# Gates of a linear-attention head by Ln and Exp in place of a reciprocal, meta scores stacked in two standing tiles, and a head's output steps regrouped, in a two-layer encoder trunk

## The chip, the cores and the metric

The kernel runs on one core of a Trainium2 chip. The metric is the device time of one execution in microseconds (us), as the median of several runs; lower is better. The core has five engines that run side by side, each through its own instructions in the order in which they were laid down: TensorE (PE in the profile; its weight loads are shown as PEld), VectorE (DVE), ScalarE (ACT), GpSimd (POOL) and SyncE (SP), which here issues the DMAs. An instruction that waits for another engine's result holds up everything behind it on its own engine.

## The reference, cut to what matters

Two encoder layers work on a residual stream of 272 positions (256 tokens and 16 learned "meta" positions) by 2048 channels. In each layer one projection gives the inputs of two head groups: four heads of bidirectional gated linear attention (GLA) and sixteen heads of neighbourhood attention (NA) on a 4 x 64 grid. Their outputs are joined, projected, added to the stream and normalised; a squared-ReLU MLP with 8192 hidden channels and another normalisation follow. All is float32.

The change touches the end of a GLA head. With o the sum of the forward and backward scans of a head (256 channels) and r the gate's projection:

```python
o = o * lax.rsqrt(jnp.mean(jnp.square(o), axis=-1, keepdims=True) + LN_EPS) * norm_w.astype(f32)
o = o.reshape(B, L, GLA_HEADS * GLA_DV) * jax.nn.silu(r.astype(f32))
```

where silu(r) = r / (1 + exp(-r)).

## The kernel before, in words

**Layout.** Channels lie on the 128 partitions, positions along the free dimension. The stream is 16 tiles of 128 channels. Layer 1 needs all 272 positions; layer 2 drops the meta positions from most products and works on 256. A float32 product is made of a high and a low part of each operand, in the type float32r: `three` (L151) issues three matmuls for each block of 128 x 128 weights in layer 1 (L160 to L162), and two, the first 512 columns wide, in layer 2 (L156, L157).

**Weights.** Weights come from HBM in tiles of 128 x 1024 (512 KB). For each tile `made` (L137) issues a DMA on SP's queue, a cast to the high part on ScalarE (`wh`, L147) and a subtraction for the low part on VectorE (`wl`, L148). There are three buffers of each kind; a tile is prepared two tiles ahead of its use.

**What sets the order.** `by_m` (L190) computes four output blocks of 128 channels (index m), each of 16 weight blocks, that is two weight tiles. After the first tile of each block and after the block's eviction it calls `pump`. `pump` (L104) feeds two queues of Python generators, a foreground queue `fg` and a background queue `bg`: each call adds a credit to each, and for every whole credit it runs one generator to its next `yield`, which lays down that step's instructions behind the weight matmuls issued so far (the `issue_after` of L98). So a *step* is the code between two yields, a *rate* is the number of steps per call of `pump`, and the small matmuls of attention stand in groups between runs of 16 or 24 projection matmuls. A generator that ends costs no credit. Within what the steps allow, the recording layer still moves single instructions a few places on an engine.

**The stage around the change**, in `layer` from L262 on. The generator `gla()` (L479) is put in `bg`. Two groups of projections (8 blocks, 16 calls of `pump`) give r for the eight gates; here the background rate is `GLA_R` = 1.3. I call this the **gate stage**. Then come six groups for NA (24 blocks); for the first five (40 calls) the background rate is `GLA_NA` = 1.1; this is the **NA stage**. Before the sixth group whatever is left of `gla()` is issued at once (L271).

- `gla()` takes two steps to start, and then for each of four heads ten *levels* and an output part. A level is a distance class of position pairs: `gaps` (L438) lets GpSimd subtract cumulated decays (four operations, L447 to L450 or L457 to L464, recorded as L460), `operands` (L467) takes Exp on ScalarE (L471) and multiplies by q and k on VectorE (L476; L473 and L474 for the last level in layer 2), and TensorE makes the scores (L505, L498 for the last), which VectorE or ScalarE puts into the head's score tile `A` (L521, L519). `gaps` runs two levels ahead of the matmul and `operands` one, with three buffers. The scores of meta positions as keys go to a tile `Am` of 16 rows (L517).
- `gla_out` (L529) makes the head's output. Step 1: a tile `am` of 80 rows is cleared on GpSimd (L533) and `stack` (L211) puts the high part of `Am` in rows 0 to 15 and 64 to 79 on ScalarE (L214, two copies) and the low part in rows 32 to 47 on VectorE (L215). Steps 2 and 3: for each half e of the head three matmuls (L542, L543 with the values V, L544 with `am`) into a PSUM bank and a Square on ScalarE (L545). Step 4: the squares are added and split (L548, L208, L209). Step 5: their mean by two matmuls (L776) and the reciprocal square root `rs` by Ln, Exp and a Newton step (`newton`, L427). It then waits, step by step, until the head's two gates are there. Steps 6 and 7: for each half VectorE computes bank x weight x `rs` (L560), then x gate (L561), and the result is split (L208, L209).
- `ev_r` (L406) evicts a projection r: exp(-r) on ScalarE (L411), + 1 on GpSimd (L412), a copy of r on ScalarE (L414). `silu` (L417), in `fg`, takes the reciprocal on VectorE in two halves (L421), a step each, and then multiplies by r (L424). With its empty first step it costs three credits.
- `na_pair` (L590), in `fg` behind them, makes two NA heads in five steps: scores (L601, L605), softmax (L582 to L588), transposes of values (L622, L623) and of probabilities (L637, L638, L640, with the evictions L641 and L642), and output (L652, L657).

Of the kernel before, what the change touches and what calls it, by code (L numbers as in the profile page):

```python
# [2 lines left out]

# [15 lines left out]
NM = 16  # L19
L = T + NM  # L20
DEPTH = 2
ROWS, GW = 4, 64
GH, GDK, GDV = 4, 128, 256
# [8 lines left out]
EPS = 1e-5  # L32
TAU = 16.0
NEG = -1e30
GLA_R, GLA_NA, NORMS = 1.3, 1.1, (1.0, 0.6)
LEAD = 4


# [9 lines left out]
class Trunk:  # L48
# [18 lines left out]
    def consts(self):  # L67
        nc, c = self.nc, self.cp
        t = lambda n, s, d=F32: c.tile(s, d, name=n, tag=n)
# [19 lines left out]
            nc.scalar.copy(self.ones_r[n], self.ones[n])  # L89
        self.eps = t("eps", [P, 1])  # L90
        nc.gpsimd.memset(self.eps, EPS)
        self.one = t("one", [P, 1])
        nc.gpsimd.memset(self.one, 1.0)

# [311 lines left out]
    def ev_r(self, c, ps):  # L406

        nc, n = self.nc, self.n
        self.y[c] = self.pair(self.yp, "y", c)
        s = self.g2.tile([P, L], F32, name="rs", tag="rs")[:, :n]  # L410
        nc.scalar.activation(s, ps, AF.Exp, scale=-1.0)  # L411
        nc.gpsimd.tensor_scalar(s, s, 1.0, 1.0, ALU.mult, ALU.add)  # L412
        r = self.g2.tile([P, L], F32, name="rv", tag="rv")[:, :n]
        nc.scalar.copy(r, ps)  # L414
        self.fg.append(self.silu(c, s, r))

    def silu(self, c, s, r):  # L417
        yield
        half = self.n // 2
        for p in (slice(0, half), slice(half, self.n)):  # L420
            self.nc.vector.reciprocal(s[:, p], s[:, p])  # L421
# [57 lines left out]
    def gla(self):  # L479
# [4 lines left out]
        nc, n, full, g2 = self.nc, self.n, self.full, self.g2  # L484
        levels = (7, 0, 1, 2, 3, 4, 5, 6, 8, 9)
        todo = iter([(h, lv) for h in range(GH) for lv in levels])
        begun = [self.gaps(*next(todo)) for _ in range(2)]
        yield
        ahead = self.operands(*begun.pop(0))
        yield  # L490
        for h in range(GH):
            A = g2.tile([P, 6, P], F32, name="A", tag="A")
            Am = g2.tile([NM, L], F32, name="Am", tag="Am")
            for lv in levels:
                q, k = ahead
                ps = self.bank()
# [17 lines left out]
                if lv == 9:  # L514
                    if full:
                        nc.vector.tensor_copy(A[:, 2:6:3, :NM], ps[:, T:T + 2 * NM].rearrange("p (s c) -> p s c", s=2))
                    nc.scalar.copy(Am[:, :T], ps[:NM, :T])  # L517
                elif lv >= 7:
                    nc.scalar.copy(A[:, 0:5:4, :] if lv == 7 else A[:, 1:4:2, :], p2)  # L519
                else:  # L520
                    nc.vector.copy_predicated(A[:, 0:5:4, :], self.mask[:, lv:lv + 1, :].to_broadcast([P, 2, P]), p2)  # L521
# [5 lines left out]
            yield from self.gla_out(h, A, Am)  # L527

    def gla_out(self, h, A, Am):  # L529

        nc, n, g2 = self.nc, self.n, self.g2
        am = g2.tile([80, L], F32R, name="am", tag="am")[:, :n]
        nc.gpsimd.memset(am.bitcast(F32), 0.0)  # L533
        self.stack(Am[:, :n], am, NM, (0, 64), 32)
        yield
        af = A.rearrange("p s c -> p (s c)")
        os_ = []
        sq = g2.tile([P, 2, L], F32, name="sq", tag="sq", bufs=1)
        for e in range(2):
# [4 lines left out]
            nc.tensor.matmul(o, lhsT=self.VS[:, c], rhs=am, start=False, stop=True)  # L544
# [478 lines left out]
```

## Time and profile before

| what | value |
|---|---|
| median of 3 runs | 2427.86 us (2427.23 to 2428.85) |
| the profiled execution's own time | 2427.82 us |
| its span, first to last instruction | 2425.8 us |
| granted TensorE clock over the span | 0.997 |
| TensorE busy | 2394.4 us (99%) |
| VectorE busy | 1576.3 us (65%) |
| ScalarE busy | 1189.2 us (49%) |
| GpSimd busy | 285.7 us (12%) |
| all DMA | 417.46 MB, 172 GB/s |
| TensorE's share of the chain that ended last | 94% |

Layer 1 runs until about 1245 us, layer 2 from there. The gate stage of layer 1 lies at about 120 to 183 us and its NA stage behind it to about 340 us; in layer 2 the two lie at about 1357 to 1411 us and 1411 to 1570 us. How to read the views: the *waits* list sums, for an engine, the idle time ahead of its instructions by the instruction that ended it; the *chain* follows the work that ended last back from the end, at each place to what released it; the *windows* give the busy time of each engine in a stretch of the span; a *group* is all instructions of one line, engine and operation, with their number and mean time. A float32 matmul that is not of the type float32r is recorded as two, so the two score products of a level appear as four L505.

### The profile page before, as it was taken

To read this page: it belongs to the slowest core of one execution; us is meant where nothing else is said; L and a number is where in the kernel's file an instruction comes from. 1 tells how busy PE (TensorE), PEld (TensorE's weight loads), DVE (VectorE), ACT (ScalarE), POOL (GpSimd) and SP (SyncE) were. 2 spreads that over 40 slices of the span, in tenths; PEclk is the share of its full clock that TensorE was granted. 3 is DMA by queue.
4 is the path that set the end of the run, shared out by engine and by line. 5 is a ranking of instruction groups with operands and counts; after the bars stand their busy time and mean duration, and the time that the engine had idled before them with its cause. 6 is when DMAs were issued, how large, how long until landed. Compare 5 with 4: busy or idle time off the path is not lost.

```text
span 2425.8 us, 43082 instructions
## 1 busy us (share of the span) xinstructions
PE 2394.4 (99%) x17276; PEld 2270.6 (94%) x17276; DVE 1576.3 (65%) x2469; ACT 1189.2 (49%) x1962; POOL 285.7 (12%) x447
## 2 busy tenths in 40 slices
PE   9999999999999999999999999999999999999997
PEld 9999999999999999999999899999988888888886
DVE  6688777775544455546577787778866555666655
ACT  6555555564433344444456555555644333444443
POOL 1064420010000000000021444300200000000000
PEclk9999999999999999999999999999999999999998
DMA  7544444555555555555555444456566556556563
GB/s 243 165 133 155 145 133 158 172 179 175 174 175 174 175 177 174 177 175 173 176 168 186 144 156 150 136 156 191 184 190 184 190 189 187 189 185 189 186 189 129
DMA packets 118359, 417.46 MB, mean 172 GB/s; under 512 B 13388, under 2 KB 16332, under 8 KB 118160
## 3 DMA queue, kind: packets, MB, share of 16 engines
q1 hardware_dynamic: 118160, 414.72, 54.1%
q8 instruction: 135, 2.21, 0.4%
q14 instruction: 64, 0.52, 0.1%
HBM read 412.57 MB, written 2.10 MB: 171 GB/s over the span
## 4 chain that ended last, share of the span: by engine, by line
PE 94%; DVE 3%; issue 1%; ACT 1%; DMA 0%; POOL 0%; SPq 0%; ACTq 0%; DVEq 0%; POOLq 0%
PE mm L156 22%; PE mm L160 17%; PE mm L162 17%; PE mm L161 17%; PE mm L157 11%; PE mm L186 5%; PE bg L505 1%; DVE wl L148 1%; PE bg L652 1%; DVE acc L868 1%; PE bg L601 0%; POOL lev L460 0%; ACT wh L147 0%; PE bg L322 0%; PE bg L542 0%
## 5 line engine op out<-in xcount | busy, mean ns | idle before, releaser
L148 DVE TENSOR_TENSOR wl<-raw,wh 128x1024 fp32r<-128x1024 f32 (+1 forms) x772 | 946.0, 1226 | 654.6 <-ACT wh L147 646.2
L147 ACT CAST wh<-raw 128x1024 fp32r<-128x1024 f32 (+1 forms) x772 | 805.1, 1044 | 956.6 <-PE mm L161 405.6
L160 PE MATMUL mm<-x,wh 128*128 128x272 f32 (+2 forms) x2176 | 632.6, 291 | 0.0
L161 PE MATMUL mm<-x,wh 128*128 128x272 f32 (+2 forms) x2176 | 628.4, 289 | 0.0
L162 PE MATMUL mm<-x,wl 128*128 128x272 f32 (+2 forms) x2176 | 628.4, 289 | 0.0
L160 PEld LDWEIGHTS mm<-x,wh 128*128 128x128 f32 x2176 | 413.3, 190 | 1.4 <-issue 0.5
L162 PEld LDWEIGHTS mm<-x,wl 128*128 128x128 f32 x2176 | 410.6, 189 | 0.3
L161 PEld LDWEIGHTS mm<-x,wh 128*128 128x128 f32 x2176 | 410.0, 188 | 0.1
L156 PE MATMUL mm<-x,wh 128*128 128x512 f32 x1152 | 408.7, 397 | 0.0
L157 PE MATMUL mm<-x,wl 128*128 128x256 f32 x1152 | 324.5, 282 | 0.3 <-DVE wl L148 0.3
L156 PEld LDWEIGHTS mm<-x,wh 128*128 128x128 f32 x1152 | 217.7, 189 | 49.8 <-issue 0.6
L156 PE MATMUL mm<-y,wh 128*128 128x512 f32 x704 | 248.2, 393 | 0.1
L157 PEld LDWEIGHTS mm<-x,wl 128*128 128x128 f32 x1152 | 217.6, 189 | 0.8 <-DVE wl L148 0.8
L162 PE MATMUL mm<-y,wl 128*128 128x272 f32 x704 | 203.2, 289 | 0.0
L160 PE MATMUL mm<-y,wh 128*128 128x272 f32 x704 | 203.2, 289 | 0.0
L161 PE MATMUL mm<-y,wh 128*128 128x272 f32 x704 | 202.9, 288 | 0.0
L157 PE MATMUL mm<-y,wl 128*128 128x256 f32 x704 | 197.6, 281 | 0.5 <-DVE wl L148 0.5
L156 PE MATMUL mm<-u,wh 128*128 128x512 f32 x512 | 180.6, 393 | 0.0
L460 POOL TENSOR_TENSOR lev<-be 128x128 f32<-128x128 f32 (+1 forms) x256 | 151.9, 623 | 117.9 <-PE bg L505 49.8
L156 PEld LDWEIGHTS mm<-y,wh 128*128 128x128 f32 x704 | 131.8, 187 | 30.5 <-ACT wh L147 0.5
L162 PE MATMUL mm<-u,wl 128*128 128x272 f32 x512 | 147.8, 289 | 0.0
L160 PE MATMUL mm<-u,wh 128*128 128x272 f32 x512 | 147.8, 289 | 0.0
(234 smaller groups left out, 3327.9 us busy)
## 6 DMA issues: line engine op xcount, KB each, us to landing
raw<-in_wff SPq DMA_DIRECT2D x512, 512.0 KB, 3.6
raw<-in_win SPq DMA_DIRECT2D x190, 512.0 KB, 3.5
raw<-in_wout SPq DMA_DIRECT2D x64, 512.0 KB, 3.6
nb<-in_nab SPq DMA_DIRECT2D x16, 352.0 KB, 3.3
out<-acc SPq DMA_DIRECT2D x8, 256.0 KB, 2.2
xraw<-in_xT SPq DMA_DIRECT2D x7, 272.0 KB, 5.2
wraw<-in_wup SPq DMA_DIRECT2D x2, 392.0 KB
raw<-in_win SPq DMA_DIRECT2D x4, 128.0 KB, 2.8
```

Source lines behind the costliest of these rows:

```text
L147: nc.scalar.copy(wh[:, c], raw[:, c])
L148: self.wl = nc.vector.tensor_tensor(wl[:, c], raw[:, c], wh[:, c].bitcast(F32), ALU.subtract).ins
L156: mm(ps, lhsT=wh[:, c:c + P], rhs=x.both[:, :, :T], start=first, stop=False)
L157: mm(ps[:, T:], lhsT=wl[:, c:c + P], rhs=xh[:, :T], start=False, stop=last)
L160: mm(o, lhsT=wh[:, c:c + P], rhs=xh[:, :n], start=first, stop=False)
L161: mm(o, lhsT=wh[:, c:c + P], rhs=xl[:, :n], start=False, stop=False)
L162: mm(o, lhsT=wl[:, c:c + P], rhs=xh[:, :n], start=False, stop=last)
L186: self.nc.tensor.matmul(ps[m][:, :n], lhsT=parts[p][0][:, c:c + P], rhs=acts[j][parts[p][1]][:, :n], start=j + p == 0, stop=j == nk - 1 an ...
L460: tt = lambda o, x, y: nc.gpsimd.tensor_tensor(o, x, y, ALU.subtract)
L505: nc.tensor.matmul(ps[:, b], lhsT=k[:, b], rhs=q[:, r], start=True, stop=True)
L652: nc.tensor.matmul(r[hs], lhsT=(v2 if rest else v1)[:, t, hs], rhs=p2[:, t, :] if rest else p1[:, 2 * t + hh, :], start=rest, stop=not rest)
L868: return self.nc.vector.tensor_tensor(v, v, by[:, None, :].to_broadcast([P, m, n]), alu)
```

## The change

1. Gates. exp(-r) is capped at 1e38 as 1 is added (same GpSimd operation), and r is evicted negated. `silu` then takes 1/d as Exp(-Ln(d)) on ScalarE (scaled by 2^-64 inside the Ln, undone by the bias `down`), and refines it on VectorE by one Newton step that also multiplies by r: three operations. It takes two credits.
2. Two tiles `am0`, `am1` of the whole kernel part stand for all heads and are cleared once per layer; stacking moves into the step of the last level.
3. `gla_out` waits for its two gates first. One step then issues the six matmuls (both halves' V products, then both `am` products), the two Squares, and for each half bank x weight x gate on VectorE; the banks are read for the last time here. The last two steps multiply by `rs` from SBUF. An output part has five steps in place of seven.
4. Rates: `GLA_R` from 1.3 to 0.95, `GLA_NA` from 1.1 to 1.17.

```diff
-GLA_R, GLA_NA, NORMS = 1.3, 1.1, (1.0, 0.6)
+GLA_R, GLA_NA, NORMS = 0.95, 1.17, (1.0, 0.6)
+BIG = 1e38
...
+        self.down = t("down", [P, 1])
+        nc.gpsimd.memset(self.down, -64 * math.log(2))
...
-        s = self.g2.tile([P, L], F32, name="rs", tag="rs")[:, :n]
-        nc.scalar.activation(s, ps, AF.Exp, scale=-1.0)
-        nc.gpsimd.tensor_scalar(s, s, 1.0, 1.0, ALU.mult, ALU.add)
+        d = self.g2.tile([P, L], F32, name="rd", tag="rd")[:, :n]
+        nc.scalar.activation(d, ps, AF.Exp, scale=-1.0)
+        nc.gpsimd.tensor_scalar(d, d, BIG, 1.0, ALU.min, ALU.add)
         r = self.g2.tile([P, L], F32, name="rv", tag="rv")[:, :n]
-        nc.scalar.copy(r, ps)
-        self.fg.append(self.silu(c, s, r))
-
-    def silu(self, c, s, r):
-        yield
-        half = self.n // 2
-        for p in (slice(0, half), slice(half, self.n)):
-            self.nc.vector.reciprocal(s[:, p], s[:, p])
-            yield
-        gate = self.g2.tile([P, L], F32, name=f"gate{c}", tag=f"gate{c}", bufs=1)[:, :self.n]
-        self.nc.vector.tensor_tensor(gate, r, s, ALU.mult)
-        self.gate[c] = gate
+        nc.scalar.activation(r, ps, AF.Copy, scale=-1.0)
+        self.fg.append(self.silu(c, d, r))
+
+    def silu(self, c, d, r):
+
+        yield
+        nc = self.nc
+        y = self.g2.tile([P, L], F32, name=f"gate{c}", tag=f"gate{c}", bufs=1)[:, :self.n]
+        nc.scalar.activation(y, d, AF.Ln, scale=2.0 ** -64)
+        nc.scalar.activation(y, y, AF.Exp, scale=-1.0, bias=self.down)
+        yield
+        nc.vector.tensor_tensor(d, d, y, ALU.mult)
+        nc.vector.scalar_tensor_tensor(d, d, -2.0, y, ALU.add, ALU.mult)
+        nc.vector.tensor_tensor(y, d, r, ALU.mult)
+        self.gate[c] = y
...
+        ams = [g2.tile([80, L], F32R, name=f"am{i}", tag=f"am{i}", bufs=1) for i in range(2)]
+        for am in ams:
+            nc.gpsimd.memset(am.bitcast(F32), 0.0)
...
                     nc.scalar.copy(Am[:, :T], ps[:NM, :T])
+                    am = ams[h % 2][:, :n]
+                    self.stack(Am[:, :n], am, NM, (0, 64), 32)
...
-    def gla_out(self, h, A, Am):
+    def gla_out(self, h, A, am):
...
-        am = g2.tile([80, L], F32R, name="am", tag="am")[:, :n]
-        nc.gpsimd.memset(am.bitcast(F32), 0.0)
-        self.stack(Am[:, :n], am, NM, (0, 64), 32)
-        yield
+        while 2 * h + 1 not in self.gate:
+            yield
         af = A.rearrange("p s c -> p (s c)")
-        os_ = []
         sq = g2.tile([P, 2, L], F32, name="sq", tag="sq", bufs=1)
-        for e in range(2):
-            o = self.bank()[:, :n]
-            c = slice(h * GDV + e * P, h * GDV + e * P + P)
+        os_ = [(self.bank()[:, :n], slice(h * GDV + e * P, h * GDV + e * P + P)) for e in range(2)]
+        for o, c in os_:
             nc.tensor.matmul(o, lhsT=self.V[0][:, c], rhs=af[:, :n], start=True, stop=False)
             nc.tensor.matmul(o, lhsT=self.V[1][:, c], rhs=af[:, 384:384 + n], start=False, stop=False)
+        for o, c in os_:
             nc.tensor.matmul(o, lhsT=self.VS[:, c], rhs=am, start=False, stop=True)
+        on = []
+        for e, (o, c) in enumerate(os_):
             nc.scalar.activation(sq[:, e, :n], o, AF.Square)
-            os_.append(o)
-            yield
+            t = g2.tile([P, L], F32, name="on", tag="on")[:, :n]
+            nc.vector.scalar_tensor_tensor(t, o, self.vec[:, self.l, 64 + e:65 + e], self.gate[2 * h + e],
+                                           ALU.mult, ALU.mult)
+            on.append(t)
+        yield
...
-        while 2 * h + 1 not in self.gate:
-            yield
         for e in range(2):
             c = 2 * h + e
             hi, lo = (t[:, :n] for t in self.y[c])
-            o = g2.tile([P, L], F32, name="on", tag="on")[:, :n]
-            nc.vector.scalar_tensor_tensor(o, os_[e], self.vec[:, self.l, 64 + e:65 + e], rs, ALU.mult, ALU.mult)
-            nc.vector.tensor_tensor(o, o, self.gate[c], ALU.mult)
-            self.split(o, hi, lo)
+            nc.vector.tensor_tensor(on[e], on[e], rs, ALU.mult)
+            self.split(on[e], hi, lo)
```

More of the change, by code (lines that the diff above doesn't have):

```diff
@@ L1 @@
+import math
 from collections import deque
@@ L526, in gla @@
                 yield
[L527 to L529 removed]
+            yield from self.gla_out(h, A, am)
+    def gla_out(self, h, A, am):
         nc, n, g2 = self.nc, self.n, self.g2
[L532 to L535 removed]
+        while 2 * h + 1 not in self.gate:
+            yield
         af = A.rearrange("p s c -> p (s c)")
[L537 removed]
         sq = g2.tile([P, 2, L], F32, name="sq", tag="sq", bufs=1)
[L539 to L541 removed]
+        os_ = [(self.bank()[:, :n], slice(h * GDV + e * P, h * GDV + e * P + P)) for e in range(2)]
+        for o, c in os_:
             nc.tensor.matmul(o, lhsT=self.V[0][:, c], rhs=af[:, :n], start=True, stop=False)
             nc.tensor.matmul(o, lhsT=self.V[1][:, c], rhs=af[:, 384:384 + n], start=False, stop=False)
+        for o, c in os_:
             nc.tensor.matmul(o, lhsT=self.VS[:, c], rhs=am, start=False, stop=True)
+        on = []
+        for e, (o, c) in enumerate(os_):
             nc.scalar.activation(sq[:, e, :n], o, AF.Square)
[L546 to L547 removed]
+            t = g2.tile([P, L], F32, name="on", tag="on")[:, :n]
[3 more added lines that the diff above has]
+        yield
         nc.vector.tensor_tensor(sq[:, 0, :n], sq[:, 0, :n], sq[:, 1, :n], ALU.add)
```

## The prediction

> **What bounds the kernel now.** I read the page first, for the engines' shares:
>
> ```profile
> span 2425.8 us, 43082 instructions
> PE 2394.4 (99%) x17276; PEld 2270.6 (94%) x17276; DVE 1576.3 (65%) x2469; ACT 1189.2 (49%) x1962; POOL 285.7 (12%) x447
> ```
>
> TensorE is busy for all but 31.4 us, and the change takes no matmul from it. The time can fall only by idle time of TensorE, and only where the change reaches: gate and NA stage. So next came the windows of these stages: bounds, length, then busy time of TensorE, weight loads, VectorE, ScalarE and GpSimd. Layer 1 first (two lines), then layer 2:
>
> ```profile
> 120.00:183.00 63.00, 61.94 (x493) 61.25 (x493) 51.33 (x79) 31.95 (x55) 42.38 (x61) 1.00 0.43 137
> 183.00:340.00 157.00, 156.90 (x1316) 153.01 (x1316) 120.75 (x267) 90.62 (x214) 66.53 (x115) 1.00 0.45 146
> 1357.00:1411.00 54.00, 50.15 (x299) 43.56 (x298) 46.16 (x70) 31.22 (x57) 30.28 (x51) 1.00 0.46 143
> 1411.00:1570.00 159.00, 157.28 (x1201) 146.65 (x1199) 122.63 (x227) 90.92 (x199) 72.17 (x121) 1.00 0.47 147
> ```
>
> TensorE's idle time is 1.06 and 0.10 us in layer 1, 3.85 and 1.72 us in layer 2; the worst stage is the one where VectorE is busy for 46.16 of 54 us. The waits of TensorE in layer 2 (1344 to 1600 us) name the places:
>
> ```profile
> PE bg L544 <- ACT rs L411: 1.7, 1, 1.7
> PE bg L505 <- DVE lev L476: 1.2, 2, 1.0
> PE bg L652 <- DVE p L642: 0.8, 1, 0.8
> PE bg L776 <- ACT sp L208: 0.8, 1, 0.8
> PE bg L498 <- ACT rv L414: 0.6, 1, 0.6
> PE mm L157 <- DVE wl L148: 0.3, 1, 0.3
> ```
>
> Each is one event or two. Layer 1 has a single one, 1.06 us ahead of L544. An idle stretch costs more than itself, since the matmuls' overlap starts anew: from the matmul before to the one after, the V products that waited 1.06 us took 2.47 us and the same group without a wait 1.17, so 1.30 for 1.06. I add 0.2 us to each event (an estimate from this pair). Last, the chain at two of the places. Layer 2, the wait ahead of L505 at 1369.89 us:
>
> ```profile
> 1366.26 1.42 DVE wl L148
> 1367.68 0.86 DVE rs L421
> 1368.54 0.30 DVE A L521
> 1368.84 0.30 DVE jn L170
> 1369.14 0.61 DVE lev L476
> ```
>
> VectorE works without a pause, a reciprocal in the middle, and the level's operand L476 comes late. Layer 1, the wait ahead of L544, which starts at 153.77:
>
> ```profile
> 148.76 3.41 POOL lev L460 x4
> ...
> 152.75 0.41 ACT am L214
> ...
> 153.19 0.44 DVE am L215
> ```
>
> The stacking of `am` stands on ScalarE behind an Exp (L471, at 152.19) that waits for GpSimd.
>
> **The change part by part.**
>
> *Stacking.* Four of the eight clearings (L533, 0.32 us each on GpSimd) go, and stacking starts one step earlier. After the last level's matmul it needs ScalarE's Exp of the next level (L471, 0.63), `Am` (L517, 0.36), two copies (L214, 2 x 0.40) and the low part (L215, 0.42): 2.2 us, about 2.5 with the hand-overs. Where the V products come a whole call of `pump` later, TensorE covers this with 16 projection matmuls in layer 2 (eight pairs of 0.35 us by the starts of neighbours: 2.8 us) and four V products of 0.46 us each: 4.6 us. So the waits ahead of L544 go: 1.06 + 1.71 + 2 x 0.2 = **3.2 us**. The built order shows one head in each layer (the second) where the last level and the V products fall into one call; the cover there is 1.84 us and three or four projection matmuls, 2.2 to 2.5 us. Each can wait 0 to 1 us; I take 0.4 each, **+0.8**.
>
> *Gates and the gate stage's rate.* A gate now costs VectorE two reciprocals (L421, median 0.953) and a product (L424, 0.434): 2.34 us. New are three operations like L424, L432 and L561 (0.43): 1.29 us, so 16.8 us less over 16 gates. ScalarE gets Ln and Exp, priced by L429 and L430 at 0.42 to 0.48, so 0.9 us a gate and 14 us in all; it has 23 us free in layer 2's gate stage. The lower rate takes 16 x 0.35 = 5.6 steps out of that stage, each level 0.69 (L476) + 0.44 (L521) on VectorE: 6.3 us. VectorE then needs about 38 us there (46.2 - 6.3, less some 2 for seven or eight gates at 1.29 in place of five at 2.34), and TensorE 47.9 (50.15 less five levels of 0.45): 79% in place of 85%, with no level pair in one call, which was the case in the chain above. I let the waits on L476, L414 and L148 go (1.02 + 0.18 + 0.60 + 0.34, and 4 x 0.2: 2.9 us) but for 0.6 us: **-2.3**. If ScalarE's new pair holds up the weight casts instead, that is the slower rival. VectorE's relief is worth nothing by itself in layer 1, where TensorE hides it all.
>
> *A head's values in one step.* VectorE's count and kinds stay (L560, L561); ScalarE's Squares too. The banks come free some steps earlier; no wait of TensorE in the list is put down to L560, so that is worth 0. The six matmuls in a row cover the two PSUM reads (0.49 each). The mean's matmuls L776 waited 0.77 us and then 0.08 at 1447 us, where the split and the mean fell into one call of `pump`; in the new order no such pair is left. 0.85 and two restarts: **-1.2 us**. The wait for the gates ahead of the V products costs nothing: the second gate is there after about six calls, the first head ends after twelve.
>
> *More in the NA stage.* The foreground backlog of eight credits is gone (24 credits against 16 calls before, 16 now), so NA pairs start eight calls earlier, and their bias loads on SP's queue too; DMA engines are 0.47 busy, and no wait names them. Two starting steps, 40 levels and 20 output steps are 62, and the credits are 15.2 + 46.8 = 62, so the six steps that were issued at once ahead of the sixth group are spread; they had cost TensorE nothing. But calls with two level steps in the NA stage rise from two to five in layer 2. One such pair led to the wait of L652 (0.80): GpSimd's seven L460 in a row (4.13 us) held up an Exp, that the cast, that L148, that L642. In the new order these pairs stand where no transposes follow in the next call, so that event may go (-1.0 with its restart) or repeat (0.5 a pair by one event in two pairs, 3 more: +1.5). I take the middle, **+0.3**.
>
> *Fewer, longer groups.* A level standing alone adds 0.36 us to the projection's run (0.49 less the 0.126 of a projection matmul), behind another small group 0.45. Seven groups fewer: 7 x 0.09 = **+0.6**.
>
> Sum: -3.2 + 0.8 - 2.3 - 1.2 + 0.3 + 0.6 = **-5.0 us**. Against the profiled execution's 2427.82 that is 2422.8; its median differs by 0.04, so I leave it there.
>
> A rule that speaks against the change: the three new operations read two SBUF tensors each, the reciprocal one. In this trace L424, of that kind, goes from 0.415 to 0.675 us, and L412 on GpSimd from 0.404 to 1.397. The Trainium skill (GPSIMD Engine Reference, Specifications) says that GpSimd shares its SBUF interfaces with VectorE and contends with instructions that have two SBUF inputs; the spread of these rows agrees.
>
> **The rivals.**
>
> *Contention eats the relief (unchanged within 0.2%).* At 0.675 each, the new operations cost 2.0 us a gate and save 0.3. Then only the lower rate helps, and I keep half of the 2.3; GpSimd's levels get slower too, and the pair event repeats (+1.5 for +0.3): -5.0 + 1.15 + 1.2 = -2.65, **2425.2**. For it: 0.675 occurs. Against it: the median is 0.434, and GpSimd's share falls with the rate.
>
> *Waits return in the NA stage (also within 0.2%).* Stacking waits 1 us in both heads (+1.2 more) and the pair event repeats (+1.2 more): -5.0 + 2.4 gives **2425.2** as well. Against it: layer 1's pairs in the NA stage never idled TensorE.
>
> *All idle time goes.* The events are 6.56 us (1.06 + 1.71 + 1.20 + 0.80 + 0.85 + 0.60 + 0.34) and 9 restarts of 0.2: 8.4; less 0.6 for the groups, **2420.0**.
>
> *ScalarE becomes the bound: slower.* Ln waits for GpSimd's add, which stands behind a level's four L460 (2.58 us at 1523.95); behind Ln on ScalarE stands the next weight tile's cast. It decides from where the add ends more than about 2.8 us, half a projection block, after the eviction. At 1.5 us of starved TensorE for each of layer 2's eight gates, +12 - 5.0: **2435**. For it: ScalarE waits for L460 eight times in that stage, 11.0 us, up to 2.4. Against it: no wait of TensorE there went back to those, tiles are two ahead, and at 0.95 GpSimd has 2.0 to 2.9 us of level work for each 3.2 us call.
>
> That Ln and Exp would reload tables I leave out as a case: L429 and L430 alternate so already, and the trace has one ACT_TABLE_LOAD (1.28 us).
>
> **How the numbers follow.** About 0.2% (4.9 us) is what a measurement here can tell from no change. Forecast, -5 us and the neighbourhood down to all idle time gone: 0.50 for faster. The two rivals within 0.2%, and the forecast missed by a little: 0.43. ScalarE's bound: 0.07. The likeliest is 2422.8. The range takes in all idle time gone (2420.0) and, upward, the rivals at 2425.2 with the gate stage's 2.3 lost too: 2427.5.
>
> **What would show it.** In the new profile: no wait of TensorE ahead of L544 but in second heads; VectorE under 85% in layer 2's gate stage; TensorE's idle time there 1 us or less in place of 3.85; no L776 wait near 0.8. A wait of L156 or L157 on the cast or on L148 within the gate stage would show ScalarE's bound. New waits of L505 or L652 in calls with two levels would show the NA stage's. I am wrong if idle time in these stages stays at 6 us, or if TensorE's busy time moves by more than 1 us.

## The result and the profile after

The changed kernel takes **2439.18 us** (median of 4 runs, 2438.83 to 2439.64); the kernel before, beside it, 2427.55 (2427.09 to 2428.85). The ratio is 1.0047, 95% interval 1.003 to 1.0065: slower by 11.6 us. The forecast was 2422.8, so it is missed in sign and by 16 us.

The page of the profiled execution after: the span, the engines' busy times, and the shares of the chain that ended last.

```profile
span 2437.5 us, 43085 instructions
...
PE 2396.9 (98%) x17276; PEld 2273.1 (93%) x17276; DVE 1564.4 (64%) x2469; ACT 1199.8 (49%) x1994; POOL 302.6 (12%) x444
...
PE 89%; DVE 4%; POOL 3%; issue 2%; ACT 1%; DMA 0%; SPq 0%; ACTq 0%; POOLq 0%; DVEq 0%
```

The span is 11.7 us longer: TensorE's idle time rose from 31.4 to 40.6 us (+9.2) and its busy time by 2.5. VectorE lost 11.9 us of work, ScalarE gained 10.6, and GpSimd gained 16.9 although it has three instructions less (444 for 447). TensorE's share of the chain fell from 94 to 89%, and GpSimd, at 12% of the span, holds 3% of it. The windows of the same stretches as before show where:

```profile
120.00:183.00 63.00, 61.34 (x480) 60.13 (x479) 47.65 (x79) 39.04 (x73) 45.10 (x56) 1.00 0.42 138
183.00:340.00 157.00, 154.59 (x1286) 150.04 (x1285) 116.94 (x265) 88.33 (x212) 76.20 (x124) 1.00 0.43 139
1357.00:1411.00 54.00, 45.91 (x259) 39.27 (x257) 37.64 (x60) 31.51 (x63) 32.60 (x44) 0.97 0.43 141
1411.00:1570.00 159.00, 154.71 (x1164) 144.53 (x1162) 122.45 (x226) 93.28 (x203) 76.05 (x127) 1.00 0.46 145
```

TensorE's idle time in the four is 1.66, 2.41, 8.09 and 4.29 us, where it was 1.06, 0.10, 3.85 and 1.72: +9.7, where the whole span has +9.2. VectorE's share in layer 2's gate stage did fall, to 37.64 of 54 us, 70%. (The stretch is the same, but the projection matmuls that filled it before now run from 1360.95 to 1419.60 us; over these, VectorE is busy for 43.38 of 58.65 us, 74%.) So VectorE got its relief, and TensorE waited more.

Most of the rise in busy time goes with the waits too. The granted clock of the third line is 0.97 because of one stretch at half the clock, right behind TensorE's longest wait in the four (3.90 us), which ended at 1405.62 us. Here is that stretch, and then one of the same length behind it (the granted clock is the third number from the end):

```profile
1406.63:1410.04 3.41, 3.41 (x13) 2.93 (x12) 2.67 (x5) 2.26 (x6) 0.57 (x1) 0.50 0.23 71
1410.04:1413.45 3.41, 3.41 (x22) 3.01 (x21) 1.89 (x6) 2.44 (x5) 0.50 (x1) 1.00 0.35 144
```

In it TensorE runs 13 matmuls where it then runs 22; a pair of projection matmuls takes 0.64 us from start to start where it then takes 0.35. That is about 1.7 us lost (an estimate, half of 3.41), the greater part of the 2.5. The kernel before has no such stretch except over the last 16 us of the span, where all the kernels have one. In the traces of all 20 kernels here, each wait of TensorE of 2.0 us or more in these stages has a stretch at half the clock around or behind it, 3.41 or 6.83 us long; of the waits from 1.75 to 1.96 us some have one; shorter ones have none, the longest of before (1.71 us) among them.

The waits of TensorE in layer 2 (1344 to 1600 us):

```profile
PE bg L553 <- DVE am L219: 5.8, 2, 3.9
PE mm L161 <- DVE wl L152: 3.2, 3, 1.8
PE bg L662 <- DVE p L652: 2.4, 3, 1.1
PE bg L550 <- ACT A L531: 1.0, 1, 1.0
```

Lines have moved: the `am` product L544 is now L553, `wl` L152, the subtractions L460 are L467, GpSimd's step of a gate L412 is L416, Ln and Exp of a gate are L426 and L427, an output of NA L662. Projection matmuls in the gate stage now wait for the weights' low part, as the prediction's slower rival would have it, and the `am` products wait in layer 2's first two heads. Two chains explain the two kinds. First the wait of 1.84 us ahead of L161 at 1382 us:

```profile
1376.93 2.50 POOL lev L467 x4
...
1379.46 0.64 ACT lev L478
...
1380.12 0.94 DVE lev L483
1381.06 0.56 DVE rd L429
...
1382.73 0.33 DVE jn L174
1383.06 1.15 DVE wl L152
```

It starts with a level's subtractions on GpSimd; their Exp, the product, and then the gate's three operations and the weights' low part follow. Second, the wait of 1.86 us of layer 2's second head, from 1456.9 us on:

```profile
1454.77 2.46 POOL lev L467 x4
...
1457.26 0.63 ACT lev L478
1457.88 0.30 ACT am L218
...
1458.21 0.43 DVE am L219
```

Here the subtractions of a later level stand ahead of the stacking: ScalarE has that level's Exp ahead of the two `am` copies in its order, and waits for it. Both begin on GpSimd, so I looked at GpSimd's own order. Its timeline in layer 2's gate stage (in brackets the idle time before an instruction and what ended it):

```profile
1366.59 1.26 POOL L416 TENSOR_SCALAR rd<-rd 128x256 f32<-128x256 f32 x1 [1.06 <-ACT rd L415]
1367.93 4.44 POOL L467 TENSOR_TENSOR lev<-be 128x128 f32<-128x128 f32 x8
1375.78 1.07 POOL L416 TENSOR_SCALAR rd<-rd 128x256 f32<-128x256 f32 x1 [3.41 <-ACT rd L415]
1376.93 4.39 POOL L467 TENSOR_TENSOR lev<-be 128x128 f32<-128x128 f32 x8
1383.60 1.52 POOL L416 TENSOR_SCALAR rd<-rd 128x256 f32<-128x256 f32 x1 [2.27 <-ACT rd L415]
```

GpSimd idles 3.41 us with subtractions queued, since the gate's step stands ahead of them and waits for an eviction; and the step then takes 1.07 us or more. The subtractions at 1376.93 are those of the first chain. The matmul that freed the buffer of the first four of them had ended at 1372.39 us, 4.5 us earlier.

### The profile page after: what moved, and what is told of

Read it like the earlier page. It is cut to its first block, busy times and chain, and to the rows that moved or that the text cites. A ratio compares the mean times of both kernels' runs of the same rounds, so it can differ in the third digit from the quotient of the medians.

```text
span 2437.5 us, 43085 instructions
## 1 busy us (share of the span) xinstructions
PE 2396.9 (98%) x17276; PEld 2273.1 (93%) x17276; DVE 1564.4 (64%) x2469; ACT 1199.8 (49%) x1994; POOL 302.6 (12%) x444
## 4 chain that ended last, share of the span: by engine, by line
PE 89%; DVE 4%; POOL 3%; issue 2%; ACT 1%; DMA 0%; SPq 0%; ACTq 0%; POOLq 0%; DVEq 0%
PE mm L160 21%; PE mm L164 16%; PE mm L166 16%; PE mm L165 16%; PE mm L161 11%; PE mm L190 6%; POOL lev L467 2%; DVE wl L152 1%; PE bg L515 1%; DVE acc L878 1%; PE bg L662 1%; PE bg L611 0%; PE bg L326 0%; ACT ns L594 0%; ACT wh L151 0%
## 5 line engine op out<-in xcount | busy, mean ns | idle before, releaser
L152 DVE TENSOR_TENSOR wl<-raw,wh 128x1024 fp32r<-128x1024 f32 (+1 forms) x772 | 946.4, 1227 | 663.0 <-ACT wh L151 654.4
L161 PE MATMUL mm<-x,wl 128*128 128x256 f32 x1152 | 325.2, 282 | 3.2 <-DVE wl L152 3.2
L161 PEld LDWEIGHTS mm<-x,wl 128*128 128x128 f32 x1152 | 218.1, 189 | 4.2 <-DVE wl L152 4.2
L161 PE MATMUL mm<-y,wl 128*128 128x256 f32 x704 | 197.9, 282 | 0.5 <-DVE wl L152 0.5
L467 POOL TENSOR_TENSOR lev<-be 128x128 f32<-128x128 f32 (+1 forms) x256 | 157.3, 646 | 82.7 <-DVE be L351 45.5
```

The lines of the kernel that those rows point to most:

```text
L152: self.wl = nc.vector.tensor_tensor(wl[:, c], raw[:, c], wh[:, c].bitcast(F32), ALU.subtract).ins
L161: mm(ps[:, T:], lhsT=wl[:, c:c + P], rhs=xh[:, :T], start=False, stop=last)
L467: tt = lambda o, x, y: nc.gpsimd.tensor_tensor(o, x, y, ALU.subtract)
```

## The experiments

Each run was compared with the kernel before on the same chip (2427.4 to 2427.9 us there), so times of runs from different chips compare to within about 0.5 us. All of them:

| run | base | time, us | ratio, 95% interval |
|---|---|---|---|
| e1 old rates | after | 2445.76 | 1.0077 (1.0062 to 1.0092) |
| e2 old gates | after | 2431.38 | 1.0015 (1.0006 to 1.0025) |
| e3 new gates only | before | 2439.34 | 1.005 (1.0035 to 1.0065) |
| e5 new rates only | before | 2429.75 | 1.001 (1.0 to 1.0019) |
| f1 gates without a GpSimd step | e3 | 2427.02 | 0.9997 (0.9987 to 1.0006) |
| f2 no refinement on VectorE | e3 | 2438.43 | 1.0046 (1.003 to 1.0062) |
| f3 a third credit | e3 | 2437.05 | 1.0041 (1.0025 to 1.0056) |
| f4 reciprocal, two credits | before | 2436.39 | 1.0036 (1.0022 to 1.005) |
| g1 idle step, min and add | f1 | 2437.90 | 1.0041 (1.0026 to 1.0056) |
| g2 no GpSimd step | after | 2431.42 | 1.0015 (1.0006 to 1.0024) |
| g5 stacking ahead of Exp | g2 | 2425.84 | 0.9991 (0.9982 to 1.0001) |
| g6 the reciprocal a call later | f4 | 2433.48 | 1.0023 (1.0014 to 1.0033) |
| h1 mult for min | after | 2435.10 | 1.003 (1.0018 to 1.0042) |
| h2 mult for min | e3 | 2437.54 | 1.0037 (1.0023 to 1.0052) |
| h3 idle step, mult and add | g1 | 2432.08 | 1.0015 (1.0006 to 1.0025) |
| h4 old rates | g5 | 2430.54 | 1.0011 (1.0002 to 1.002) |
| i1 stacking ahead of Exp | after | 2435.96 | 1.0034 (1.0021 to 1.0047) |
| i2 idle step, mult and add | g2 | 2435.09 | 1.0029 (1.0019 to 1.004) |

The intervals are about 2 to 4 us to either side, as wide as some of the differences below. What supports these is that the times of the two runs' executions don't overlap, except where it is said.

### Which part: the gates, the rates, or the rest

**e1**, the old rates in the changed kernel:

```diff
-GLA_R, GLA_NA, NORMS = 0.95, 1.17, (1.0, 0.6)
+GLA_R, GLA_NA, NORMS = 1.3, 1.1, (1.0, 0.6)
```

> The changed kernel with the rates of before (1.3 and 1.1). Two theories for the 11.6 us. A, the gates: Ln on ScalarE stands behind GpSimd's add and ahead of the weight casts, so that the gate stage loses time whatever the rate. B, the NA stage: its higher rate puts level pairs and attention pairs into the same calls, and the last level and the V products of a head into one call, and L553 and L662 wait there. A: 2438 to 2442, no better, since more levels share the gate stage with the gates. B: about 2433, since the NA stage's idle time (6.7 us in the changed kernel, 1.8 before) goes back to about 2 us.

**e2**, the old gates in the changed kernel (its `ev_r` and `silu` are those of before):

```diff
-        nc.scalar.activation(y, d, AF.Ln, scale=2.0 ** -64)
-        nc.scalar.activation(y, y, AF.Exp, scale=-1.0, bias=self.down)
...
+            self.nc.vector.reciprocal(s[:, p], s[:, p])
```

> The changed kernel with the gates of before: reciprocal on VectorE in two halves, three credits a gate; new stacking, new output step and new rates stay. A (gates on ScalarE): about 2430, the gate stage's wait of L161 on the low part of the weights goes. B (NA stage): 2434 to 2437, the waits of L553 and L662 in the NA stage stay.

**e3**, the kernel before with the changed `ev_r` and `silu` and nothing else:

```diff
-            self.nc.vector.reciprocal(s[:, p], s[:, p])
...
+        nc.scalar.activation(y, d, AF.Ln, scale=2.0 ** -64)
+        nc.scalar.activation(y, y, AF.Exp, scale=-1.0, bias=self.down)
```

> The kernel of before with the new gates alone. A (gates on ScalarE): 2432 to 2436, with new waits on the low part of the weights in layer 2's gate stage. B (NA stage): 2424 to 2428, the relief of VectorE shows.

**e5**, the kernel before with the new rates alone:

```diff
-GLA_R, GLA_NA, NORMS = 1.3, 1.1, (1.0, 0.6)
+GLA_R, GLA_NA, NORMS = 0.95, 1.17, (1.0, 0.6)
```

> The kernel of before with the new rates alone (0.95 and 1.17), so that 8 of 70 background steps are left to be issued at once ahead of the sixth group. A (gates on ScalarE): 2425 to 2428, the gate stage gets lighter. B (NA stage): 2431 to 2434.

Measured: the gates alone cost 11.9 us (e3), and giving them back returns 7.8 (e2). The rates help the changed kernel by 6.6 us (e1) and cost the kernel before 2.3 (e5), where the idle time of the gate stages falls from 4.9 to 1.9 us but five outputs of NA wait for `p`:

```profile
PE bg L652 <- DVE p L642: 5.0, 5, 1.5
```

So the gates are the greater part, though not as theory A has it: its time came out in e2 alone, e1 and e3 lie above its ranges, and e5 lies between A's and B's. In e2, with the gates of before, the new stacking still makes TensorE wait for `am`, 3.67 us in layer 2's first head and 1.81 in its second (5.5 in the list; L550 is L553 there):

```profile
PE bg L550 <- DVE am L219: 5.5, 2, 3.7
```

In e3 ScalarE waits for GpSimd's step, and VectorE for ScalarE (layer 1's gate stage, 118 to 185 us):

```profile
ACT gate L426 <- POOL rd L416: 10.9, 8, 1.9
DVE rd L429 <- ACT gate L427: 7.8, 5, 3.1
```

That looked like a loop through GpSimd, closed by ScalarE's wait.

### What of the gates

**f1**, e3 with the 1 added inside Ln and inside VectorE's first operation, so that GpSimd has no step; the cap at 1e38 is left out:

```diff
-        nc.gpsimd.tensor_scalar(d, d, BIG, 1.0, ALU.min, ALU.add)
...
-        nc.scalar.activation(y, d, AF.Ln, scale=2.0 ** -64)
+        nc.scalar.activation(y, d, AF.Ln, bias=self.one)
...
-        nc.vector.tensor_tensor(d, d, y, ALU.mult)
+        nc.vector.scalar_tensor_tensor(d, d, 1.0, y, ALU.add, ALU.mult)
```

> The kernel of before with the new gates alone, but without GpSimd's step: Ln takes its + 1 as a bias, and the first of VectorE's three operations adds 1 as it multiplies. The cap at 1e38, which matters for r below about -87, is left out. The new gates alone cost 11.9 us. C, the loop: Ln on ScalarE waits for GpSimd, whose add waits for ScalarE, and the weight casts and the next levels' Exps wait behind; then 2428 to 2431, and the waits of L426 on L416 and of L416 on L415 are gone. D, ScalarE's time alone (0.9 us a gate): 2436 to 2439, nothing changes. E, the gates end a credit earlier: also 2436 to 2439.

**f2**, e3 with the refinement left out (one product on VectorE in place of three operations):

```diff
-        nc.vector.tensor_tensor(d, d, y, ALU.mult)
-        nc.vector.scalar_tensor_tensor(d, d, -2.0, y, ALU.add, ALU.mult)
-        nc.vector.tensor_tensor(y, d, r, ALU.mult)
+        nc.vector.tensor_tensor(y, y, r, ALU.mult)
```

> The kernel of before with the new gates alone, without the refinement: VectorE has one product a gate in place of three operations, so the gate has the accuracy of Ln and Exp. C (loop through GpSimd): 2435 to 2438, since ScalarE and GpSimd do what they did. F, VectorE's three operations in a row at the wrong place: 2428 to 2431. D and E: 2435 to 2438.

**f3**, e3 with a third credit, so that TensorE's order is that of before:

```diff
         nc.scalar.activation(y, y, AF.Exp, scale=-1.0, bias=self.down)
         yield
+        yield
```

> The kernel of before with the new gates alone, and one more empty step between Exp and VectorE's part, so that a gate takes three credits as before. C (loop): 2436 to 2439, the same waits. D: the same. E (a gate ends a credit earlier, so attention pairs start eight calls earlier, and VectorE waits for Exp): 2429 to 2432.

**f4**, the kernel before with both halves of the reciprocal in one step:

```diff
             self.nc.vector.reciprocal(s[:, p], s[:, p])
-            yield
+        yield
```

> The kernel of before, the reciprocal's two halves in one step, so that a gate takes two credits as in the changed kernel; no operation is added or taken away. E: 2433 to 2438. C, D and F: 2426 to 2430.

Measured: without GpSimd's step 12.3 us of e3's loss come back (f1); without two of VectorE's operations 0.9 (f2, whose times overlap with e3's), with another credit 2.3 (f3). f4 costs 9.0 us although it has the operations of before, which is what E expected; in layer 1's gate stage VectorE's reciprocals now wait 5.5 us for GpSimd's step, where it was 0.6:

```profile
DVE rs L421 <- POOL rs L412: 5.5, 8, 1.7
```

f1 does not say why the step costs: by ScalarE's wait for it, or by the step itself.

### The wait or the step

**g1**, f1 with the step back on GpSimd, on a copy of r and into a tile that nobody reads before it is written anew:

```diff
         nc.scalar.activation(r, ps, AF.Copy, scale=-1.0)
+        nc.gpsimd.tensor_scalar(self.y[c][1][:, :n], r, BIG, 1.0, ALU.min, ALU.add)
```

> The kernel before with the new gates, where Ln adds the 1 itself and so waits for nothing of GpSimd's (the cap at 1e38 is left out), but GpSimd still does an addition of the same size for every gate, on another tile, whose result nobody reads until the head's output overwrites it. Theory C1 (ScalarE's wait for the addition is what costs): the time stays at that of the run without the addition, 2426 to 2429 us. Rival C2 (GpSimd's own time costs, since the levels' subtractions come later by it): near the run with the addition in the loop, 2434 to 2439 us. In between, both take part in that ratio.

**g2**, the changed kernel with f1's gates:

```diff
-        nc.gpsimd.tensor_scalar(d, d, BIG, 1.0, ALU.min, ALU.add)
...
+        nc.scalar.activation(y, d, AF.Ln, bias=self.one)
```

> The changed kernel, with Ln adding the 1 itself, no step on GpSimd in a gate, and the cap at 1e38 left out. If the loop through GpSimd is all that the change lost: the waits of the weight casts in layer 2's gate stage go, but the waits ahead of L553 in the second heads (1.75 and 1.86 us) stay, since they come from the order on ScalarE: 2427 to 2431 us. If the stacking and the new rates have losses of their own that do not need the gates: 2434 us or more.

**g5**, g2 with ScalarE's order changed, so that a later level's Exp is recorded behind the last `am` copy:

```diff
-            self.nc.scalar.copy(dst[i:i + n], src)
+            self.stacked = self.nc.scalar.copy(dst[i:i + n], src).ins
...
-            nc.scalar.activation(t[:, :, :w], t[:, :, :w], AF.Exp, scale=1 / TAU)
+            with self.tc.issue_after(self.stacked):
+                nc.scalar.activation(t[:, :, :w], t[:, :, :w], AF.Exp, scale=1 / TAU)
```

> The run without the addition, and with the two am copies put ahead of the later levels' Exp in ScalarE's order. If the order on ScalarE is what holds the V products: the waits ahead of L553 (6 to 7 us in three events with their restarts) go, and the time is 3 to 7 us under that of the run without the addition alone, 2422 to 2426 us. If they wait for something else (GpSimd's subtractions by another way): within 2 us of that run, and the wait of L553 stays.

**g6**, f4 with an empty step ahead of the reciprocals:

```diff
         yield
+        yield
```

> The kernel before with both halves of the reciprocal in one step, as in the run that took 2436 us, but with one empty step more ahead of them, so that each gate's reciprocals come two calls after the eviction. If what costs is that the reader comes one call after the eviction and waits for GpSimd's addition: back to 2426 to 2430 us, and VectorE's waits for L412 under 1 us. If it is the 1.9 us without a pause on VectorE: 2434 to 2438 us again.

Measured: g1 takes 2437.90, so **a step that nobody reads costs 10.9 us**. My theory of the loop, that ScalarE's wait does it (C1), falls; GpSimd's own queue is what counts (C2). The order of TensorE, VectorE, ScalarE and SyncE is the same in f1 and g1 to the instruction, and no instruction of the other engines is put down as waiting for the idle step, so its place on GpSimd is the cause. g2 gives 7.8 us back in the changed kernel (to 2431.42, a little above its range), and g5 5.6 more; the waits ahead of the `am` product fall from 6.6 us in three events to 3.0 in two. In g2 (where L553 is L552) and in g5:

```profile
PE bg L552 <- DVE am L219: 6.6, 3, 3.0
```

```profile
PE bg L553 <- DVE am L219: 3.0, 2, 2.6
```

g6 gets 2.9 of f4's 9.0 us back, between the two expectations; the times of the two overlap a little.

Then a look at the durations of the step itself. The groups of L416 in the changed kernel (layer 1's and layer 2's shape):

```profile
L416 POOL TENSOR_SCALAR rd<-rd 128x272 f32<-128x272 f32 x8 | 12.0, 1498 | 76.2 <-ACT rd L415 75.8
L416 POOL TENSOR_SCALAR rd<-rd 128x256 f32<-128x256 f32 x8 | 9.7, 1208 | 57.6 <-ACT rd L415 57.6
```

The same step of before:

```profile
L412 POOL TENSOR_SCALAR rs<-rs 128x272 f32<-128x272 f32 x8 | 7.9, 986 | 20.1 <-ACT rs L411 20.0
L412 POOL TENSOR_SCALAR rs<-rs 128x256 f32<-128x256 f32 x8 | 3.9, 488 | 44.3 <-ACT rs L411 44.3
```

The shortest of the 16 take 1.067 us after and 0.404 before. One operator differs: min with 1e38 and add 1, where it was mult by 1 and add 1. (The factor 1 is nothing special: L452 in the kernel before, times 2 plus 0, takes 0.404 at the least too.) It is not only the recorded length: where the next instruction follows at once, it starts 1.15 us after the step's start at the least in the changed kernel and 0.37 in the one before.

### The operator

**h1**, the changed kernel with that operator exchanged (the cap left out); the order of every engine stays the same:

```diff
-        nc.gpsimd.tensor_scalar(d, d, BIG, 1.0, ALU.min, ALU.add)
+        nc.gpsimd.tensor_scalar(d, d, 1.0, 1.0, ALU.mult, ALU.add)
```

> The changed kernel with one operator exchanged: GpSimd's step of a gate is x * 1 + 1 in place of min(x, 1e38) + 1 (the cap is left out); the order of every engine stays the same to the instruction. Theory D (the form with min takes GpSimd at least 1.06 us where the old one, mult and add, took 0.40, and the level subtractions that stand behind it come later by that): L416 falls to 0.40 at the least, and most of the 11.6 us comes back: 2428 to 2432 us, the rest being the second heads' waits ahead of L553. Rival C1 (Ln's wait on ScalarE for any step on GpSimd): 2436 us or more, since Ln still waits. In between, both share it in that ratio.

**h2**, the same exchange, to the letter, in e3:

> The kernel before with the new gates only, which took 2439 us, with the same exchange of min for mult (the cap left out). Theory D: 2427 to 2431 us, L416 at 0.40 us at the least. Rival C1: 2436 us or more.

**h3**, the same exchange in g1's idle step:

```diff
-        nc.gpsimd.tensor_scalar(self.y[c][1][:, :n], r, BIG, 1.0, ALU.min, ALU.add)
+        nc.gpsimd.tensor_scalar(self.y[c][1][:, :n], r, 1.0, 1.0, ALU.mult, ALU.add)
```

> The run with the idle addition on GpSimd, which took 2438 us, with the same exchange of min for mult. Theory D: the idle step costs 16 times some 0.65 us less of GpSimd's time, and 2427 to 2431 us. If it is rather that any step there makes the level subtractions wait for the eviction: 2434 us or more.

**h4**, g5 with e1's edit, the rates 1.3 and 1.1:

> The run with the stacking put ahead of the later Exp and no step on GpSimd, which took 2425.8 us, with the old rates 1.3 and 1.1. If the new rates are worth what the prediction took for them in the gate stage: 2426 to 2430 us. If they cost more in the NA stage than they save once GpSimd is free: 2421 to 2424 us, which would beat both kernels.

Measured: the operator is worth 4.1 us in the changed kernel, 1.8 in e3 and 5.8 in g1. All three runs lie above Theory D's ranges, and h2 within the rival's. In h1 GpSimd's steps take 11.0 us in place of 21.7:

```profile
L416 POOL TENSOR_SCALAR rd<-rd 128x272 f32<-128x272 f32 x8 | 6.7, 839 | 76.0 <-ACT rd L415 76.0
L416 POOL TENSOR_SCALAR rd<-rd 128x256 f32<-128x256 f32 x8 | 4.3, 543 | 60.5 <-ACT rd L415 60.5
```

So Theory D holds as one cause of several, not as the cause: of g1's 10.9 us the operator makes 5.8, and any step there, even at 0.40 us, the other 5.1. The new rates are right once the rest is mended: h4 is 4.7 us slower than g5.

### The rest

**i1**, the changed kernel in full, with g5's edit alone:

> The changed kernel in full, with nothing left out, and with only ScalarE's order exchanged: the two am copies of a head stand ahead of the Exp of a later level. The same exchange gave 5.6 us back where no step of a gate stood on GpSimd. If the order is a cause of its own: 2432 to 2435 us, and the waits ahead of L553 in the two second heads (1.75 and 1.86 us) go. If it counts only once GpSimd is free: 2437 us or more.

**i2**, g2 with h3's idle step:

```diff
         nc.scalar.activation(r, ps, AF.Copy, scale=-1.0)
+        nc.gpsimd.tensor_scalar(self.y[c][1][:, :n], r, 1.0, 1.0, ALU.mult, ALU.add)
```

> The changed kernel with Ln adding the 1 itself (the cap left out), as in the run that took 2431.4 us, and with an idle step x * 1 + 1 on GpSimd for every gate, whose result nobody reads. It parts the 3.7 us that lay between the run with mult and add in the loop (2435.1) and the run without a step on GpSimd. If GpSimd's queue is held by any step that waits for the eviction: 2434 to 2436 us. If it was ScalarE's wait for the step: 2430 to 2432.5 us.

Measured: the order alone gives 3.2 us (i1, between the two expectations), less than the 5.6 that it gives without a step on GpSimd. The wait of layer 1's second head is gone, that of layer 2's is 0.4, and the first head's 3.9 stays (L554 here is L553):

```profile
PE bg L554 <- DVE am L219: 4.3, 2, 3.9
```

i2 takes what h1 takes, 2435.09 and 2435.10: in the changed kernel, Ln's wait costs nothing measurable, and the step's place in GpSimd's queue costs 3.7. (The two orders differ by a few places on three engines, and the idle step waits for the copy of r, about 0.3 us later than the Exp.) How the hold looks: GpSimd in layer 2's gate stage in i2, and then without the step in g2.

```profile
1363.11 0.92 POOL L418 TENSOR_SCALAR y<-rv 128x256 fp32r<-128x256 f32 x1 [1.36 <-ACT rv L417]
1364.00 4.75 POOL L467 TENSOR_TENSOR lev<-be 128x128 f32<-128x128 f32 x8
1372.13 0.41 POOL L418 TENSOR_SCALAR y<-rv 128x256 fp32r<-128x256 f32 x1 [3.38 <-ACT rv L417]
```

```profile
1364.28 3.04 POOL L466 TENSOR_TENSOR lev<-be 128x128 f32<-128x128 f32 x4 [1.23 <-PE bg L514]
1367.47 2.18 POOL L466 TENSOR_TENSOR lev<-be 128x128 f32<-128x128 f32 x4 [0.16 <-PE bg L514]
1370.72 2.60 POOL L466 TENSOR_TENSOR lev<-be 128x128 f32<-128x128 f32 x4 [1.08 <-PE bg L514]
```

With the step, the subtractions of two levels come together behind an eviction, here after 3.38 us of idle time; without it, those of each level shown start when a level's matmul frees their buffer.

Kernels with the same order on TensorE can be laid side by side, matmul by matmul: by how many us does the one that stands at a given place start later? At the bounds of the stages (times of the kernel compared with), from one profiled execution each (those of g2 and g5 are the slowest of their ten):

```
                  118    185    220   1344   1412   1460   2400
against f1
  h3 (mult)       0.3    1.4    0.7    0.7    5.2    5.2    5.2
  g1 (min)        0.4    1.6    2.3    2.3   10.2   11.2   10.7
against g5
  g2             -0.6   -0.7    2.8    3.0    2.0    5.0    5.4
  h1              0.4    0.9    2.8    3.0    6.7    8.3    8.2
  i1             -0.3    2.5    2.5    2.6    7.6    7.7    7.8
  after          -0.1    2.6    4.5    4.8   10.0   11.5   11.9
```

The step's cost arises in the gate stages (118 to 185 and, above all, 1344 to 1412 us) and the order's at the second heads (185 to 220 and 1412 to 1460); elsewhere these lags move by about 1 us at most. So the loss of 11.6 us is, taken off one after the other: 4.1 the operator min (2439.18 to 2435.10), 3.7 the step in GpSimd's queue (to 2431.42), 5.6 ScalarE's order at the stacking (to 2425.84); and what is then left of the change is 1.9 us under the kernel before (2427.72 beside g5), which is not told apart from nothing. The parts are not independent: the order is worth 3.2 ahead of the other two and 5.6 behind them. And the second is not the change's alone: the kernel before has a step of a gate in GpSimd's queue as well, and what it costs there was not tried.

g5 is the fastest of all, but its interval reaches 1.0001, so it isn't told apart from the kernel before, and it leaves the cap out. Without that, none beats both.

**Open:** in e3's family, h2 (Ln waits) takes 5.5 us more than h3 (nobody waits), so ScalarE's wait may cost there; but the orders of VectorE and ScalarE differ between the two. And why f4 is slow, with old operators and old steps, is settled only in part: a later start gives 2.9 back, in layer 1's gate stage alone. That the other 6 are the two reciprocals in a row on VectorE wasn't tried apart, nor was a third credit in the changed kernel. How much of each loss is the half clock behind a wait and how much the wait itself was not parted either; executions of one kernel differ in it (g5's ten: a mean clock of 0.997 in the three fastest, 0.996 in the five slowest).

## Why the prediction was wrong, point by point

**Gates and the gate stage's rate (-2.3): the step that failed.** I priced what VectorE and ScalarE would do and took GpSimd's step as unchanged. Its operator had changed, from mult to min: +9.9 us of GpSimd's time over 16 gates (21.7 for 11.8), in a queue that starts the level chain. The profile of before had a row that could have warned me: the two-operator steps L450, subtract and mult on 128 x 256 with a column in place of one constant, at 1.153 us each. The runs show what that cost: 4.1 us by the operator (h1), and 3.7 by the step's place in GpSimd's queue (i2 against g2), which I had put at nothing. That the durations on VectorE and ScalarE were about right (medians 0.443, 0.473 and 0.436 for the three operations, 0.425 and 0.509 for Ln and Exp) did not help, and neither did VectorE's 74% for the predicted 79. f2 has 14.7 us less work on VectorE than e3 with the same order on TensorE, and is 0.9 us faster, within the two runs' spread: with the new gates, VectorE's relief buys next to nothing, and what TensorE waits for in the chains above starts on GpSimd. No run parts VectorE's relief from the rest in the kernel before. The rates were tried only together. They helped more than I took for the one of the gate stage where the gates are new (6.6 us in the changed kernel, 4.7 in the mended one), and cost 2.3 in the kernel before.

**Stacking (-3.2, +0.8 for second heads).** The wait of layer 1's first head went (its V product waits 0.8 for `A` instead). That of layer 2's grew from 1.71 to 3.90 us: its chain holds GpSimd's late level, the gate's Exp, and two weight casts with their low parts. The new gates are not needed for it: the wait is 3.67 us in e2, with the old ones, and 2.95 in g2, with no step of a gate on GpSimd. The second heads waited 1.75 and 1.86 us, not 0.4: I summed Exp, `Am`, two copies and the low part to 2.2 us, and left out that this Exp itself waits for four subtractions (2.46 us), which can't start until the last level's matmul frees their buffer. The order as built showed the Exp there; I priced it as if its input were ready. i1 shows it: with the copies ahead of it, 3.2 us come back.

**A head's values in one step (-1.2).** The wait of 0.77 us ahead of the mean's matmuls went, as predicted; in layer 1 two new ones of 0.3 came. This part has no run of its own.

**More in the NA stage (+0.3).** L662 waits 2.7 us in four events, where L652 waited 0.8 in one, so it is the rival's +1.5 rather than the middle; e5 shows 5.0 us in five events from the rates alone.

**Fewer, longer groups (+0.6).** Not tried apart. TensorE's busy time rose by 2.5 us; it had been named as a sign of error from 1 us on. About 1.7 of it is the half clock behind the longest wait, so the 0.2 us that I added to each wait is too little for the long ones.

**The rivals.** The slower one, at 0.07, gave 2435 and named GpSimd's step behind a level's subtractions, and a weight cast behind Ln. The place was right, and the direction of the wait wrong: what counted was not that the step stands behind the subtractions and Ln behind it, but that later subtractions stand behind the step. My argument against it was that the lower rate leaves GpSimd 2.0 to 2.9 us of level work in a call of 3.2 us; that counts GpSimd's work and forgets its waits for the eviction, 1.06 to 4.26 us each in the profile after from 1363 to 1410 us. The rival of contention, slower steps on both engines, did not come: VectorE's three operations have the medians above in place of 0.675, and the mean of GpSimd's step lies 0.33 us above its shortest before, 0.29 after and 0.29 in h1. The Trainium skill (GPSIMD Engine Reference, 4.1 Engine selection) calls one-input elementwise work on GpSimd roughly line rate. Here the runs show two rates for one shape, 0.404 and 1.067 us, by the operator.

## What to carry to other kernels

A step on a lightly used engine is priced by its queue: ask what it waits for, what is queued behind it, and what that feeds; here a step of 0.40 us per gate that nobody read, on an engine busy for 12% of the span, cost 5.1 us in one kernel and 3.7 in another. When an edit changes an operator or a constant in an instruction that seems to stay, look for a row of that exact operator, and when a sum of durations runs through an in-order engine, ask of each instruction whether its input is ready by then. An idle copy of a suspected step, which leaves the order of the other engines the same, parts the step's own cost from the wait for its result.

## What the runs showed of the hardware

- GpSimd's two-operator step on 128 x 256 float32 takes 0.40 us at the least with mult and add, and 1.07 with min and add, in kernels whose orders are otherwise the same (h1 and the changed kernel; h3 and g1).
- Between e3 and f2 VectorE has 14.7 us less to do (1565.5 and 1550.8 us) with TensorE's order the same; the time moves by 0.9 us, which is within the runs' spread. Between h1 and the changed kernel GpSimd has 0.67 us more per gate, and the time moves by 4.1.
- TensorE's granted clock falls to a half for 3.41 or 6.83 us around or behind every wait of 2.0 us or more in the two stages (20 traces), and around or behind none of up to 1.71 us; in the changed kernel 13 matmuls then run in 3.41 us instead of 22.
